# A hybrid attention and S5 layer on one core: attention's keys and the gate products behind the top-k branch, and S5's out stage in two steps

## The chip, the cores and the metric

The kernel runs on one core of a Trainium2 chip. The metric is the device time of one execution in microseconds; the median of several runs is compared. Five engines work side by side, each through its own list of instructions in order: TensorE (PE, matmuls), VectorE (DVE), ScalarE (ACT), GpSimd (POOL) and SyncE (SP), whose queue issues nearly all of the transfers here. An instruction that waits holds up everything behind it on its own engine.

## What is computed

One inference step of a layer for a prompt of 1024 tokens and a sample of 64 tokens with a cache: a normalization modulated by a condition, one combined projection, sparse attention, a complex diagonal state space model (S5), two gates, and an output projection. Cut to what matters:

```
h = rms_norm(x, g_norm) * (1 + scale) + shift
z = h @ w_in                          # split: q k v qi ki wi ga u gs ma mb
o = attention(q, top-k of the indexer's scores)
branch_a = (o * silu(ga)) @ w_attn_proj
y = S5 scan over u, then  g_lin = gelu(y) @ w_glu
branch_b = (g_lin[:512] * sigmoid(g_lin[512:]) * silu(gs)) @ w_ssm_proj
merged = sigmoid(ma) * branch_a + sigmoid(mb) * branch_b
x = x + gate * (merged @ w_out)       # gate = the last third of silu(c) @ w_mod
```

## The kernel before

All large products are made in three passes with operands split in a high and a low part (`hhi`, `hlo` for the tokens, `whi`, `wlo` for the weights; L200, L201 and L205 are the three matmuls, ACT's L155 makes `whi` and POOL's L156 `wlo`).

The part of the combined projection that is not needed at once is held as **late work**: 32 blocks of 128 columns, each in three chunks of tokens (384, 384 and 320 wide), each chunk in three steps of eight matmuls. That is nine steps to a block and 288 in all. A chunk is collected in one of two accumulators (`acc`), and the next chunk but one can begin only when it is emptied. Who empties it depends on the block, and the blocks come in this order: four of q (ACT copies to `st`, stored in `q_d`), four of u (ACT copies to `us`, L603, stored in `u_d`), fourteen of the merge gates (ACT copies to `st`, L610, stored in `ma_d` and `mb_d`), four of attention's gate (`gate_a`: ACT's sigmoid L618, then VectorE's product L619, then POOL's product L620), four of S5's gate (`gate_s`: sigmoid, VectorE's product L628, stored), and the last two of the merge gates.

A generator hands out these steps between the steps of other work, by a table of numbers: 36 steps before top-k, one step for each of attention's 75 yields (`R_ATT`), six in the gap between attention and S5 (`N_GAP`), 3.2 for each of S5's 25 yields (`R_SSM`), three for each yield of GELU (`R_GEL`), and what is left alone. So S5 begins at step 117 and ends at step 197.

The top-k indexer ends in a branch with ten arms that only VectorE enters (`tc.If`); all engines have its branch instruction in their lists. In front of that branch the program puts the keys' layout (`build_keys`, casts L265 and L266 on ACT, L267 and L268 on VectorE) and the first query block (`att_queries`: `tab`, `qt` and `qw` loads on SP, three operations on POOL, casts to `qs` on ACT and VectorE). The order of instructions on each engine follows a scheduler that keeps data dependences and may move them past each other, so what stands behind the branch in an engine's list is to be read there.

S5 (from 509 us): four times coefficients (`eb`, L271 to L276 on VectorE) are transposed (L1360), multiplied (L1367), and the result is put into `zs`; then VectorE runs the scan, seven rounds over all states and fifteen over the carries (`cmac`, L1375 to L1379), and for each of four quarters a fix (L1414 to L1420). The out stage of a quarter (`ssm_out`) issues four transfers `zq<-zs`, multiplies (L1435, L1436), copies to `yb` and issues eight stores to `y_d`. GELU reads `y_d` back (`yt`), and its result feeds the GLU. `gates` (L1171 to L1182) multiplies the condition with the last third of `w_mod` (two loads `gw` of 2 MB), reduces it with `sel` (L1178) and stores it; it is woven with GELU.

Of the kernel before, what the change touches and what calls it, by code (L numbers as in the profile page):

```python
# [47 lines left out]


N_PRE = 6  # L50
N_TOPK = 0
R_ATT = 1.0
R_SSM = 3.2
N_GAP = 6
R_GEL = 3.0
N_ATT = 14
BO = (7, 3, 4, 5, 6, 2, 1, 0, 8)
# [25 lines left out]
def hybrid_step(ctx, tc, ins, outs):  # L83
# [50 lines left out]

    acol = small.tile([P, KD, 2], F32, name="acol")
    shcol = small.tile([P, KD, 2], F32, name="shcol")
    scs = small.tile([P, KD, 2], F32, name="scs")
    nhalf = small.tile([P, 1], F32, name="nhalf")
    pool.memset(nhalf, -0.5)
    nbig = small.tile([P, 1], F32, name="nbig")  # L140
# [301 lines left out]
    for b in range(2):  # L442
        silu = act.activation(scs[:, :, b], tp[:, 0, 8 * b:8 * b + 8], AF.Silu)
    c4 = small.tile([P, KD, 4], F32R, name="c4")
    dve.tensor_copy(c4[:, :, 0:2], scs)
    c_rest = dve.tensor_tensor(c4[:, :, 2:4], scs, c4[:, :, 0:2].bitcast(F32), op=OP.subtract)

    def chain(*gens):
        for g in gens:
# [2 lines left out]
    def run(gen):  # L452
        for _ in gen:
            pass
# [8 lines left out]

    cz = sxp.tile([P, KD, 4], F32, name="cz", bufs=1)
    pool.memset(cz, 0.0)
    dve.tensor_copy(cz[:, :, 0:2], scs)
    scr = rb.tile([P, 6, 512], F32, tag="t1", name="scr")
    params = ssm_params(ssu)
    next(params)
# [196 lines left out]
    vst = kvp.tile([P, 8, 2, 2, 64], F32R, tag="v", name="vst")  # L666
    vnew = kvp.tile([64, 2, 64], F32, name="vnew")

    atq = at_ctx.enter_context(tc.tile_pool(name="atq", bufs=2, side="right"))
    tk_ctx, ix_ctx = ExitStack(), ExitStack()  # L670
    tkp = tk_ctx.enter_context(tc.tile_pool(name="tkp", bufs=1, side="right"))
    ixp = ix_ctx.enter_context(tc.tile_pool(name="ixp", bufs=2, side="right"))
# [448 lines left out]
    def steps(fn, ts):  # L1121
        for t in ts:
            fn(t)
            yield
# [31 lines left out]
    def gates():  # L1156


        sel = small.tile([P, 2], F32, name="sel")
        for b in range(2):  # L1160
            dve.tensor_reduce(sel[:, b:b + 1], ident.rearrange("p (g r) -> p g r", r=32)[:, :, b],
                              axis=mybir.AxisListType.X, op=OP.add)
        for h in range(2):
            cols = slice(2 * D + h * 512, 2 * D + h * 512 + 512)
            ps = bank1()
            w = tokp.tile([P, KD, 512], F32, tag="wtok", name="gw")
            sync.dma_start(w, w_mod[:, cols].rearrange("(k p) c -> p k c", p=P))
            yield
            for k in range(KD):
                g = 32 * (k % 4)  # L1170
                pe.matmul(ps[g:g + 2], scs[:, k, :], w[:, k], start=(k < 4), stop=(k >= 4), skip_group_check=True)  # L1171
            yield
            r = wpool.tile([P, 528], F32, tag="raw", name="grow", bufs=RAW)[:, :512]
            pool.memset(r, 0.0)
            for g in range(0, P, 32):
                act.copy(r[g:g + 2], ps[g:g + 2])
            o = bank1()[0:2]
            pe.matmul(o, sel, r, start=True, stop=True)  # L1178
            bm = wpool.tile([P, 528], F32, tag="raw", name="gbias", bufs=RAW)[0:2, :512]
            sync.dma_start(bm, ins["b_mod"][:, cols].to_broadcast([2, 512]))  # L1180
            dve.tensor_tensor(bm, o, bm, op=OP.add)
            sync.dma_start(gate_d[:, h * 512:h * 512 + 512], bm)  # L1182
            yield
# [13 lines left out]
    for _ in range(N_TOPK):  # L1197
        next(late)
    tk = topk(ixp)
    for _ in range(N_COUNT - 1 + len(BLOCKS) + 1):  # L1200
        next(tk)

    qw = wpool.tile([P, 4, P], F32, tag="ub", name="qw", bufs=1)
    pool.memset(qw, 0.0)
# [1 line left out]
    build_keys(kst, None, [(ktok[:, t], P) for t in range(8)])  # L1206
    with tc.issue_after(q_stored.ins):
        ready = att_queries(BO[0])
    run(tk)
    rest_on[0] = pool  # L1210
    ix_ctx.close()
    tk_ctx.close()

    atp_ctx = ExitStack()
    atp = atp_ctx.enter_context(tc.tile_pool(name="atp", bufs=2, side="right"))
# [206 lines left out]
    def ssm_out(q):  # L1422
        cs, tq = ca_t[q], tq_t[q]
        rs = slice(4 * q, 4 * q + 4)
        zq = ssp.tile([P, 4, 2, NCH], F32, tag="eq", name="zq")
        for j in range(2):
            for g2 in range(2):
                sync.dma_start(zq[64 * j:64 * j + 64, :, g2, :], z4[64 * g2:64 * g2 + 64, j, rs, 0:NCH])
        yb = ssp.tile([P, 8, NCH], F32, tag="yb", name="yb")
        for g0, ng in ((0, 3), (3, 3), (6, 2)):  # L1430
            ps = bank1()
            for i in range(ng):
                g = g0 + i
                o = ps[:, i * NCH:(i + 1) * NCH]
                pe.matmul(o, tq[:, g, :], uall[:, 8 * q + g, :], start=True, stop=False)  # L1435
                pe.matmul(o, cs[:, g // 2, g % 2, :], zq[:, g // 2, g % 2, :], start=False, stop=True)  # L1436
            act.copy(yb[:, g0:g0 + ng, :], ps[:, :ng * NCH].rearrange("p (g n) -> p g n", n=NCH))
        yv = y_d[P * q:P * q + P].rearrange("(g c) t n -> c g t n", c=16)
        for t in range(8):
            sync.dma_start(yv[:, :, t, :], yb[16 * t:16 * t + 16])  # L1440

    def ssm():
        for q in range(4):
            if q == 0:
                with tc.issue_after(last_mm[0].ins):
                    ssm_in(q)
            else:
                ssm_in(q)
            yield
        for i, _ in enumerate(ssm_scan()):  # L1450
            if i == OT:
                ssm_out_tables(0)
            yield
        for q in range(4):
            ssm_fix(q)
            yield
            if q < 3:
                ssm_out_tables(q + 1)
            ssm_out(q)
            yield  # L1460

    for _ in range(N_GAP):
# [20 lines left out]
    def gelu(m):  # L1483
# [4 lines left out]
        act.activation(gt[:, 1024:TOK].rearrange("p (n t) -> p t n", t=8), yt[:, :, 0:8], AF.Gelu_apprx_tanh)  # L1488
        dve.tensor_copy(ghi[:, m], gt)
        dve.tensor_tensor(glo[:, m], gt, ghi[:, m].bitcast(F32), op=OP.subtract)  # L1490
    weave(both(steps(gelu, range(4)), gates()), late, R_GEL)
    run(late)
    hT_stack.close()

# [194 lines left out]
```

## Time and profile before

| | us |
|---|---|
| median of 3 runs | 1095.76 |
| lowest, highest | 1094.28, 1097.64 |
| the profiled execution | 1094.43 |
| its span | 1092.6 |
| TensorE busy | 991.7 |
| VectorE busy | 672.8 |
| ACT busy | 461.0 |
| POOL busy | 292.2 |

The span is the time between the first and the last instruction that the profile shows; the execution takes 1.8 us more. Busy time is the sum over an engine's instructions. A busy engine can still be slow: TensorE's clock has two levels, and the profile tells the granted clock of a stretch as a share of the full one. Idle time of TensorE is put down to what released it, in the views of waits and in brackets behind an instruction in the timeline.

### The profile page before, as it was taken

What the parts mean: (1) busy time and instruction counts of PE and PEld (TensorE: products, weight loads), DVE (VectorE), ACT (ScalarE), POOL (GpSimd) and SP (SyncE); (2) the same over time, 40 slices, a digit from 0 to 9 for tenths busy, and PEclk for the clock granted to TensorE, in tenths of its full rate; (3) what the DMA queues carried; (4) which work ended last, traced back from release to release, by engine and by line L of the source; (5) the groups of instructions that cost most, each with busy time, mean ns of one, the idle gap of its engine ahead of it and who ended that gap; (6) DMA issues with size and microseconds to landing.
All of it is one profiled execution on the core that took longest, in us unless ns stands there. A gap on an engine that the chain in (4) does not pass through costs nothing. (4 is left out here: it accounts for less than half of the span.)

```text
span 1092.6 us, 16667 instructions
## 1 busy us (share of the span) xinstructions
PE 991.7 (91%) x5948; PEld 898.3 (82%) x5948; DVE 672.8 (62%) x1426; ACT 461.0 (42%) x979; POOL 292.2 (27%) x434
## 2 busy tenths in 40 slices
PE   7777999996599999999899799847999999999997
PEld 1576878996588999988789789817999999998786
DVE  6764888899688887775689950004111656665243
ACT  3675667221476676664232022126222345442122
POOL 3574202613123221211528072303312300001211
PEclk9698999998699999999999989968999999999999
DMA  8631201122122221224733265572322345544143
GB/s 301 208 91 30 76 1 53 48 81 76 40 50 68 57 49 40 80 65 86 117 87 93 53 152 126 121 233 81 92 87 94 106 129 154 162 137 145 44 145 111
DMA packets 141766, 108.41 MB, mean 99 GB/s; under 512 B 32894, under 2 KB 128680, under 8 KB 141680
## 3 DMA queue, kind: packets, MB, share of 16 engines
q1 hardware_dynamic: 140160, 105.05, 34.6%
q10 hardware_dynamic: 1232, 2.23, 0.6%
q8 instruction: 47, 0.77, 0.3%
q14 instruction: 39, 0.32, 0.1%
q0 software_dynamic: 288, 0.05, 0.0%
HBM read 77.79 MB, written 25.17 MB: 94 GB/s over the span
## 5 line engine op out<-in xcount | busy, mean ns | idle before, releaser
L200 PE MATMUL acc<-hhi,whi 128*128 128x384 f32 (+1 forms) x768 | 257.7, 340 | 24.8 <-ACT us L603 17.4
L201 PE MATMUL acc<-hlo,whi 128*128 128x384 f32 (+1 forms) x768 | 254.5, 335 | 0.0
L200 PEld LDWEIGHTS acc<-hhi,whi 128*128 128x128 f32 x768 | 147.6, 192 | 28.6 <-ACT us L603 17.7
L156 POOL TENSOR_TENSOR wlo<-raw,whi 128x512 fp32r<-128x512 f32 x64 | 88.1, 1392 | 253.4 <-ACT whi L155 187.3
L205 PE MATMUL acc<-hhi,wlo 128*128 128x384 f32 (+1 forms) x768 | 150.7, 334 | 0.3 <-POOL wlo L156 0.3
L201 PEld LDWEIGHTS acc<-hlo,whi 128*128 128x128 f32 x768 | 147.5, 192 | 1.7 <-issue 1.0
L205 PEld LDWEIGHTS acc<-hhi,wlo 128*128 128x128 f32 x768 | 130.6, 190 | 1.6 <-POOL wlo L156 0.6
L610 ACT COPY st<-acc 128x384 f32<-128x384 f32 (+1 forms) x60 | 27.6, 461 | 120.1 <-PE acc L205 108.2
L1071 DVE TENSOR_TENSOR pt<-tp,pt 128x512 fp32r<-128x512 f32 (+3 forms) x112 | 57.3, 519 | 15.0 <-ACT pt L1070 13.7
L1050 ACT ACTIVATE pm<-pm,mx 128x1024 f32<-128x1024 f32 (+8 forms) x72 | 56.1, 779 | 21.6 <-DVE mx L1043 21.2
L155 ACT CAST whi<-raw 128x512 fp32r<-128x512 f32 x64 | 37.5, 620 | 63.0 <-DMA raw<-in_w_in 39.2
L1070 ACT CAST pt<-tp 128x512 fp32r<-128x512 f32 (+3 forms) x112 | 49.4, 451 | 31.7 <-PE tp L1066 30.6
L1624 POOL TENSOR_TENSOR yh<-yh,gfin 128x512 f32<-128x512 f32 (+1 forms) x9 | 11.6, 1289 | 173.3 <-ACT xr L1620 173.3
L200 PE MATMUL acc<-wohi,mhi 128*128 128x512 f32 (+2 forms) x152 | 56.7, 377 | 0.0
L201 PE MATMUL acc<-wolo,mhi 128*128 128x512 f32 (+2 forms) x152 | 56.6, 377 | 0.0
L1066 PE MATMUL tp<-ident,pm 128*128 128x128 f32 (+2 forms) x328 | 53.7, 271 | 2.9 <-DVE pt L1071 2.8
L1043 DVE CUSTOM_DVE_ANT_0 pm<-sc,bias 128x512 f32<-128x512 f32 (+4 forms) x72 | 42.8, 594 | 15.7 <-PE sc L1040 13.8
L1040 PE MATMUL sc<-kst,qs 128*128 128x512 f32 (+3 forms) x192 | 51.8, 357 | 0.0
L619 DVE TENSOR_TENSOR sg<-acc,sg 128x384 f32<-128x384 f32 (+1 forms) x12 | 6.4, 536 | 73.6 <-DMA zq<-zs 38.8
L1083 PE MATMUL o<-pt,vst 128*128 128x256 f32 x288 | 49.1, 295 | 0.6 <-ACT pt L1070 0.3
L1066 PEld LDWEIGHTS tp<-ident,pm 128*128 128x128 f32 (+2 forms) x328 | 38.7, 140 | 10.1 <-DVE pt L1071 5.6
L707 DVE SCALAR_TENSOR_TENSOR sc<-relu,wi,sc 128x512 f32<-128x512 f32 (+5 forms) x42 | 42.6, 1017 | 3.8 <-ACT relu L705 1.0
(483 smaller groups left out, 2271.1 us busy)
## 6 DMA issues: line engine op xcount, KB each, us to landing
raw<-in_w_in SPq DMA_DIRECT2D x68, 256.0 KB
wm<-in_w_mod SPq DMA_DIRECT2D x16, 512.0 KB
xt<-in_x_prompt SPq DMA_DIRECT2D x8, 512.0 KB
gw<-in_w_mod SPq DMA_DIRECT2D x2, 2048.0 KB
raw<-in_w_out SPq DMA_DIRECT2D x16, 256.0 KB
xr<-in_x_prompt SPq DMA_DIRECT2D x16, 256.0 KB
ma_d<-st SPq DMA_DIRECT2D x16, 192.0 KB
mb_d<-st SPq DMA_DIRECT2D x16, 192.0 KB
```

Source lines behind the costliest of these rows:

```text
L156: rest_on[0].tensor_tensor(lo, raw, hi.bitcast(F32), op=OP.subtract)
L200: pe.matmul(ps, lhi(k), rhi(k), start=(k == 0), stop=False)
L201: pe.matmul(ps, lhi(k), rlo(k), start=False, stop=False)
L205: last_mm[0] = pe.matmul(ps, llo(k), rhi(k), start=False, stop=(k == nk - 1))
L707: dve.scalar_tensor_tensor(scores[b][:nq], r[:nq, :n], w, scores[b][:nq], op0=OP.mult, op1=OP.add, accum_out=sums[:nq, 0, col] if h == 4 e ...
L1040: pe.matmul(ps, self.st[:, self.h // 2, self.h % 2, :nq], self.keys[:, self.h // 4, j, c:c + m], start=(j == 0), stop=(j == 1))
L1043: dve.tensor_tensor_reduce(out=self.pm[:, c:c + m], in0=ps, in1=bias[self.b][:nq, c:c + m], op0=OP.add, op1=OP.min, scale=-0.125, scalar=t ...
L1050: act.activation(self.pm, self.pm, AF.Exp, bias=self.ng, scale=-1.0, accum_out=self.sm)
L1066: pe.transpose(tp[:rows, i, :nq], self.pm[:, c0:c0 + rows], ident[:nq, :nq])
L1070: act.copy(d0, tp[:rows, i0:i1, :nq])
L1071: dve.tensor_tensor(d1, tp[:rows, i0:i1, :nq], d0.bitcast(F32), op=OP.subtract)
L1083: last_mm[0] = pe.matmul(o, v[:rows, kt, pr // 2].rearrange("p a d -> p (a d)"), pk[:rows, j, i, :, :nq], start=(kt == 0 and j == 0), stop ...
```

## The change

Attention's keys and first query block are no longer put in front of the top-k branch but behind it: the branch is run to its end first, its pools are closed, and then 19 late steps follow in three groups of 6, 9 and 4 (`N_BR`). Between these groups `gates()` is advanced by three and two yields; its first yield, with the first `gw` load, comes right ahead of top-k. Six late steps stand ahead of top-k (`N_TOPK`). The pool of the query tiles (`atq`) is opened after those of the branch are closed. The gate product takes 32 stationary columns (of which 30 are zero) in place of 2, so that one ACT copy of 128 partitions replaces four copies and a memset. Attention hands out 1.15 late steps per yield, the gap 12, and `ssm_out` yields once between its transfers and its matmuls, so S5 has 29 yields. GELU is woven with late steps alone. S5 now begins at step 159 and ends at step 251.

```diff
-N_TOPK = 0
-R_ATT = 1.0
+N_TOPK = 6
+N_BR = (6, 9, 4)
+R_ATT = 1.15
-N_GAP = 6
+N_GAP = 12
...
-    scs = small.tile([P, KD, 2], F32, name="scs")
+    scs = small.tile([P, KD, 32], F32, name="scs")
+    pool.memset(scs, 0.0)
...
-                pe.matmul(ps[g:g + 2], scs[:, k, :], w[:, k], start=(k < 4), stop=(k >= 4), skip_group_check=True)
+                pe.matmul(ps[g:g + 32], scs[:, k, :], w[:, k], start=(k < 4), stop=(k >= 4), skip_group_check=True)
             yield
             r = wpool.tile([P, 528], F32, tag="raw", name="grow", bufs=RAW)[:, :512]
-            pool.memset(r, 0.0)
-            for g in range(0, P, 32):
-                act.copy(r[g:g + 2], ps[g:g + 2])
+            act.copy(r, ps)
...
     tk = topk(ixp)
-    for _ in range(N_COUNT - 1 + len(BLOCKS) + 1):
-        next(tk)
+    gate_steps = gates()
+    next(gate_steps)
+    run(tk)
+    ix_ctx.close()
+    tk_ctx.close()
+    atq = at_ctx.enter_context(tc.tile_pool(name="atq", bufs=2, side="right"))
+    for n, half in zip(N_BR, (3, 2, 0)):
+        for _ in range(n):
+            next(late)
+        for _ in range(half):
+            next(gate_steps, None)
 
     qw = wpool.tile([P, 4, P], F32, tag="ub", name="qw", bufs=1)
...
         ready = att_queries(BO[0])
-    run(tk)
-    rest_on[0] = pool
-    ix_ctx.close()
-    tk_ctx.close()
...
                 sync.dma_start(zq[64 * j:64 * j + 64, :, g2, :], z4[64 * g2:64 * g2 + 64, j, rs, 0:NCH])
+        yield
         yb = ssp.tile([P, 8, NCH], F32, tag="yb", name="yb")
...
-            ssm_out(q)
+            yield from ssm_out(q)
...
-    weave(both(steps(gelu, range(4)), gates()), late, R_GEL)
+    weave(steps(gelu, range(4)), late, R_GEL)
```

**ACT behind the branch, before.** The casts of the keys (`kst`) stand in front of the evictions of the `us` blocks; two of them wait for VectorE. Numbers behind a name tell buffers apart.

```order
L970 UNCONDITIONAL_BRANCH
L155 CAST whi_4162<-raw_4164 128x512 [waits DMAHW1_49,PE_49,Pool_49]
L155 CAST whi_4162<-raw_4168 128x512 [waits DMAHW2_49]
L610 COPY st_2719<-acc_2694 128x320 [waits DMAHW7_49,PE_49,Activation_49]
L265 CAST kst_2858<-tp_2859 64x512 [waits PE_49]
L266 CAST kst_2858<-tp_2859 64x512
L265 CAST kst_2858<-tp_2872 64x512 [waits PE_49]
L266 CAST kst_2858<-tp_2872 64x512
L265 CAST kst_2858<-tp_2859 64x512 [waits DVE_49]
L266 CAST kst_2858<-tp_2859 64x512
L265 CAST kst_2858<-tp_2872 64x512 [waits DVE_49]
L266 CAST kst_2858<-tp_2872 64x512
```

**ACT behind the branch, after.** The same stretch of ACT's list in the changed kernel; the last row empties the accumulator of the chunk `acc_4109`.

```order
L971 UNCONDITIONAL_BRANCH
L157 CAST whi_2748<-raw_2750 128x512 [waits DMAHW2_49,PE_49,Pool_49]
L157 CAST whi_2748<-raw_2754 128x512 [waits DMAHW3_49]
L612 COPY st_2717<-acc_2692 128x320 [waits DMAHW0_49,PE_49,Activation_49]
L605 COPY us_2745<-acc_2720 128x384 [waits DMAHW1_49,PE_49,Activation_49]
L605 COPY us_2783<-acc_2758 128x384 [waits DMAHW4_49,PE_49,Activation_49]
L157 CAST whi_4167<-raw_4169 128x512 [waits DMAHW7_49,PE_49,Pool_49]
L157 CAST whi_4167<-raw_4173 128x512 [waits DMAHW0_49]
L254 CAST qs_4385<-qt_4374 64x4x128 [waits DVE_sequencer_49,DVE_49,Pool_49]
L605 COPY us_4134<-acc_4109 128x256 [waits DMAHW5_49,PE_49,Activation_49]
```

What moved: the casts of the keys are gone from here, two evictions have come ahead, and a cast of the first query block now stands in front of the third. It waits for POOL, which in its turn waits for VectorE's sequencer and for loads.

**VectorE at the last fix of S5, before.** The second half of the last quarter's fix (`zs`, `fin`), and the first two products of `gate_a`, which empty `acc_8538` and `acc_8592`.

```order
L1414 TENSOR_TENSOR f0_8376<-car_6943,arf_6936 128x544
L1415 TENSOR_TENSOR f1_8377<-car_6943,arf_6936 128x544 [waits DVE_49]
L1416 TENSOR_TENSOR zs_6935<-zs_6935,f0_8376 128x4x136 [waits DVE_49]
L1417 TENSOR_TENSOR zs_6935<-zs_6935,f1_8377 128x4x136 [waits DVE_49]
L1418 COPY fin_6934<-zs_6935 128x2x4 [waits DVE_49]
L1419 COPY fin_6934<-zs_6935 128x2x4
L1420 MEMSET zs_6935 128x2x4 [waits DVE_49]
L619 TENSOR_TENSOR sg_8578<-acc_8538,sg_8578 128x384 [waits DMAHW4_49,DMAHW3_49,DMAHW5_49,DMAHW1_49,DMAHW7_49,DMAHW0_49,Activation_49]
L619 TENSOR_TENSOR sg_8636<-acc_8592,sg_8636 128x384 [waits DMAHW5_49,DMAHW2_49,DMAHW6_49,DMAHW1_49,Activation_49]
```

**VectorE at the last fix of S5, after.** From the first operation of the last quarter's fix on, in the changed kernel.

```order
L1418 TENSOR_TENSOR f0_8976<-car_7361,arf_7354 128x544
L621 TENSOR_TENSOR sg_8218<-acc_8178,sg_8218 128x384 [waits DMAHW3_49,DMAHW2_49,DMAHW7_49,DMAHW1_49,Activation_49]
L1422 COPY fin_7352<-zs_7353 128x2x4 [waits DVE_49]
L1423 COPY fin_7352<-zs_7353 128x2x4
L1419 TENSOR_TENSOR f1_8977<-car_7361,arf_7354 128x544
L1424 MEMSET zs_7353 128x2x4 [waits DVE_49]
L1420 TENSOR_TENSOR zs_7353<-zs_7353,f0_8976 128x4x136
L1421 TENSOR_TENSOR zs_7353<-zs_7353,f1_8977 128x4x136 [waits DVE_49]
L621 TENSOR_TENSOR sg_8272<-acc_8232,sg_8272 128x384 [waits DMAHW4_49,DMAHW0_49,Activation_49]
```

What moved: the first products of `gate_a` now stand inside the fix of the last quarter, behind the scan and the other three fixes; before they stand behind all of it.

**TensorE at the third chunk of `gate_a`, before.** The chunk `acc_8640` takes the accumulator that `acc_8538` had; two matmuls of the third out stage stand in front of it.

```order
L201 MATMUL acc_8592<-hlo_108,whi_8408 128x384
L1435 MATMUL tp_8318<-uall_6925,tq_8139 128x136 [waits DMAHW4_49,DMAHW3_49,DMAHW5_49,DMAHW2_49,DMAHW6_49,DMAHW1_49,DMAHW7_49,DMAHW0_49,PE_49]
L1435 MATMUL tp_8326<-uall_6925,tq_8139 128x136 [waits PE_49]
L205 MATMUL acc_8592<-hhi_107,wlo_8409 128x384 x8
L200 MATMUL acc_8640<-hhi_107,whi_8408 128x320 [waits DVE_49]
```

**TensorE at the third chunk of `gate_a`, after.** The chunk `acc_8276` takes the accumulator that `acc_8178` had.

```order
L202 MATMUL acc_8232<-hhi_108,whi_8079 128x384
L203 MATMUL acc_8232<-hlo_109,whi_8079 128x384
L207 MATMUL acc_8232<-hhi_108,wlo_8080 128x384 x8
L202 MATMUL acc_8276<-hhi_108,whi_8079 128x320 [waits DVE_49]
L203 MATMUL acc_8276<-hlo_109,whi_8079 128x320
```

What moved: in TensorE's list these rows stand 19 chunks behind attention's last matmuls and in front of all of S5's out stages; before, the blocks of `gate_a` begin behind the first two out stages.

## Rows read from the trace of the kernel before

**Rows 1.** The page's first part: busy us, share of the span, instructions.

```profile
PE 991.7 (91%) x5948; PEld 898.3 (82%) x5948; DVE 672.8 (62%) x1426; ACT 461.0 (42%) x979; POOL 292.2 (27%) x434
```

**Rows 2.** Waits of TensorE, 240:320, 500:560, 610:640, 700:756: sum, times, longest.

```profile
PE acc L200 <- ACT us L603: 17.4, 1, 17.4
PE acc L200 <- ACT st L610: 3.3, 1, 3.3
...
PE tp L1360 <- DVE eb L276: 5.0, 3, 2.9
...
PE tp L1436 <- DMA zq<-zs: 8.7, 2, 6.2
...
PE tp L1171 <- DMA gw<-in_w_mod: 12.3, 2, 9.2
PE tp L1436 <- DMA zq<-zs: 4.0, 1, 4.0
PE acc L200 <- ACT whi L155: 3.8, 1, 3.8
```

**Rows 3.** Stretches: length, busy (instructions) by engine, granted clock, DMA share, GB/s.

```profile
263.00:267.50 4.50, 4.50 (x18) 4.23 (x16) 4.50 (x9) 0.73 (x2) 0.00 (x0) 0.62 0.79 219
...
741.40:747.20 5.80, 5.72 (x18) 5.72 (x19) 2.63 (x2) 2.04 (x4) 4.16 (x3) 0.50 0.43 139
```

**Rows 4.** Timeline of TensorE: start, length, line, operation, [idle before <- releaser].

```profile
509.04 1.67 PE L205 MATMUL acc<-hhi,wlo 128*128 128x384 f32 x8
...
555.01 1.57 PE L205 MATMUL acc<-hhi,wlo 128*128 128x384 f32 x8
...
566.98 0.51 PE L205 MATMUL acc<-hhi,wlo 128*128 128x384 f32 x2
```

**Rows 5.** Timeline of SP, ACT and VectorE from the last out stage to GELU.

```profile
715.53 3.64 SPq L1440 DMA_DIRECT2D y_d<-yb  x8
...
739.02 2.34 SPq L1485 DMA_DIRECT2D yt<-y_d  x2
...
746.18 2.10 ACT L1487 ACTIVATE gt<-yt 128x1024 f32<-128x1024 f32 x1
...
751.34 0.73 DVE L1489 CAST ghi<-gt 128x1088 fp32r<-128x1088 f32 x1 [0.85 <-ACT gt L1488]
752.10 1.29 DVE L1490 TENSOR_TENSOR glo<-gt,ghi 128x1088 fp32r<-128x1088 f32 x1
```

**Rows 6.** Timeline of VectorE and ACT at the end of the branch.

```profile
281.26 0.68 DVE L267 TENSOR_TENSOR kst<-tp,kst 64x512 fp32r<-64x512 f32 x1 [3.23 <-issue]
...
281.98 0.58 ACT L265 CAST kst<-tp 64x512 fp32r<-64x512 f32 x1 [18.24 <-DVE kst L267]
```

**Rows 7.** Timeline of SP and POOL: the first query block, load to use.

```profile
263.79 0.37 SPq L1005 DMA_DIRECT2D qt<-q_d  x1
...
267.72 1.77 POOL L1012 TENSOR_TENSOR qt<-qt,tab 128x512 f32<-128x512 f32 x1 [5.20 <-DMA qt<-q_d]
...
270.79 1.26 POOL L1013 TENSOR_TENSOR qt<-qt,qw 128x512 f32<-128x512 f32 x1
```

**Rows 8.** Timeline of VectorE: scan, carries, first operations of the first and last fix.

```profile
555.20 1.23 DVE L1375 TENSOR_TENSOR t<-zs,arf 128x544 f32<-128x544 f32 x1 [4.16 <-ACT zs L1371]
...
560.17 1.23 DVE L1375 TENSOR_TENSOR t<-zs,arf 128x544 f32<-128x544 f32 x1
...
565.09 2.07 DVE L1375 TENSOR_TENSOR t<-zs,arf 128x544 f32<-128x544 f32 x1
...
600.40 0.23 DVE L1375 TENSOR_TENSOR t<-car,arf 128x32 f32<-128x32 f32 x1
...
615.79 0.72 DVE L1414 TENSOR_TENSOR f<-car,arf 128x544 f32<-128x544 f32 x1
...
634.26 0.76 DVE L1414 TENSOR_TENSOR f<-car,arf 128x544 f32<-128x544 f32 x1
```

**Rows 9.** The stretch of scan and fixes: columns as in rows 3.

```profile
555.20:635.00 79.80, 71.07 (x425) 69.67 (x425) 78.14 (x143) 14.54 (x29) 34.12 (x27) 0.94 0.31 84
```

More of the change, by code (lines that the diff above doesn't have):

```diff
@@ L444, in hybrid_step @@
     c4 = small.tile([P, KD, 4], F32R, name="c4")
-    dve.tensor_copy(c4[:, :, 0:2], scs)
-    c_rest = dve.tensor_tensor(c4[:, :, 2:4], scs, c4[:, :, 0:2].bitcast(F32), op=OP.subtract)
+    dve.tensor_copy(c4[:, :, 0:2], scs[:, :, 0:2])
+    c_rest = dve.tensor_tensor(c4[:, :, 2:4], scs[:, :, 0:2], c4[:, :, 0:2].bitcast(F32), op=OP.subtract)
     def chain(*gens):
@@ L465, in hybrid_step @@
     pool.memset(cz, 0.0)
-    dve.tensor_copy(cz[:, :, 0:2], scs)
+    dve.tensor_copy(cz[:, :, 0:2], scs[:, :, 0:2])
     scr = rb.tile([P, 6, 512], F32, tag="t1", name="scr")
@@ L667, in hybrid_step @@
     vnew = kvp.tile([64, 2, 64], F32, name="vnew")
-    atq = at_ctx.enter_context(tc.tile_pool(name="atq", bufs=2, side="right"))
     tk_ctx, ix_ctx = ExitStack(), ExitStack()
```

## The prediction

> **What bounds the kernel now.** I read the page's busy times first: TensorE is busy 991.7 of 1092.6 us [rows 1], so the end is set by its work plus the time it loses. The change adds no product: the same 288 late steps (eight matmuls each, nine steps to a block of 128 columns) and the same sixteen gate products are placed elsewhere, the latter with 32 stationary columns instead of 2 and as many moving columns. So the whole question is what TensorE loses in waits and at half clock, before and after. I read that from the waits of TensorE in four stretches, then from the granted clock in the stretches behind each wait.
>
> In A, behind the top-k branch (250 to 318 us), it idles 22.6 us: 17.4 for the eviction of a `us` block on ACT, 3.3 for a `st` eviction [rows 2], and 1.9 in a smaller wait. In B, the start of S5 (509 to 556), about 7.1, of which 5.0 for the coefficient tiles `eb` of VectorE [rows 2]. In C, the first out stage (620 to 636), 8.7 for the carried states `zq` [rows 2]. In D, the end of S5 with the gate products woven into GELU (704 to 754), 25.0: 12.3 for the gate weights, 4.0 for `zq`, 3.8 for a weight cast [rows 2], and 4.9 in two smaller waits, both at the gate's reduction. Sum 63.4 us.
>
> After each pause the clock is at its lower level (1.2 GHz) for a while: ten stretches, of which the first and the last stand in [rows 3]. Busy time times (1 - granted clock) gives 4.5 x 0.38 = 1.7 and 5.72 x 0.50 = 2.9 for these two, and read the same way 6.1 for A, 1.7 for B, 2.8 for C and 9.2 for D, 19.8 in all. So before loses 28.7 in A, 8.8 in B, 11.5 in C, 34.2 in D: **83.2 us**, the most that the change can win.
>
> **C and D: the gain.** The gate products leave D for the place behind the branch, so 12.3 + 4.9 us of waits go; their loads (2 MB each) are now issued before top-k and behind the branch. `zq` was issued right before the matmuls that read it; now a yield lies between. A block of nine late steps, three column chunks, takes 566.98 - 555.01 = 11.97 us [rows 4]: 4.22 for each chunk of 384 columns, 3.53 for that of 320. By the order of the instructions four to five chunks, 16 to 21 us, lie between a quarter's fix and the matmuls that read its `zq`; the longest wait was 6.2 [rows 2]. I cost C at nothing: the cover is these chunks. If it went, 6 to 9 us would come back.
>
> D has a new price. The late steps are used up earlier (19 at the branch, 86 instead of 75 in attention, 12 instead of 6 in the gap, 92 instead of 80 in S5), so behind the last out stage only six chunks, 24 us, stand in front of the GLU, against 33 before. Its input comes by a chain: eight `y_d` stores (3.6 us to issue), the `yt` load (issued at 739.02, used by ACT at 746.18, so 7.2), then four GELU blocks of 2.1 + 0.3 on ACT, and the cast and the split of the last (0.73 + 1.29) on VectorE [rows 5]. The stores wait for `yb` and the first loads also stand behind two `ma`/`mb` stores on SP's queue. That makes 30.5 to 32 us against 24 to 26: a wait of some 6, and 2 at half clock. D: 34.2 becomes **8** (3 to 12).
>
> **A: one wait for another.** The keys' casts no longer stand on ACT in front of the `us` evictions, which is what made TensorE wait: ACT waited 18.24 us for VectorE's L267, and that stood behind the branch (L267 starts at 281.26, with 3.23 us of issue before it) [rows 6]. But the first query block is moved as well, and its tiles come from a pool that is opened only after the branch's pools are closed. So SP's `tab` load now waits for the branch. Queued behind it on SP are the `qt` and `qw` loads, the `u_d` stores and the next weights; on ACT the cast `qs<-qt` stands in front of the eviction that TensorE needs (the order shows it). The chain: the branch's end at 278 to 281.3; load to use 267.72 - 263.79 = 3.9; three operations on POOL to 270.79 + 1.26, that is 4.3 [rows 7]; a cast 0.6 and the eviction 0.4. TensorE resumes at 287.5 to 291, I take 290.7 (the end of the issue time in [rows 6]). It runs dry later than now (267.5), by one chunk of 3.5, one of 4.2 and half of the gate products, 1.7: at 277. So 13.8 idle (10.5 to 15) in place of 17.4, and as before 3.3 and 1.3 ahead of it, about 6 at half clock; 1.9 may go or stay. A: 28.7 becomes **26** (22 to 31). The second query block's casts stand in front of the next eviction too; with two accumulators TensorE has 8 to 11 us of cover for a chain of the same 10 to 11, so I take nothing for it.
>
> **B and the scan: the new wait.** With 12 steps ahead and 92 in S5, the blocks of `gate_a` (late steps 198 to 234) come inside S5; in before S5 ended at step 197. Their eviction needs VectorE (the product at L619, `sg<-acc`), and the order shows the first such product behind seven rounds of the long scan, fifteen of the carries, the fixes of three quarters and the first operation of the fourth. TensorE has two accumulators: it must wait with the third `gate_a` chunk until VectorE comes to that product. When? In before VectorE reached the same operation at 634.26 to 635.0, with TensorE's last attention matmuls at 509.04 [rows 4, 8]: +126, and the product +0.6. VectorE's start of the scan (555.20, +46) is set by `par` and by TensorE's transposes; by the after order I get +45, so it stays. TensorE's work in after from attention's end to that chunk: 13 chunks x 4.22 + 6 x 3.53 = 76, transposes and small products 15: 91. So TensorE waits 126.5 - 91 = **35** of which about 3 fall at S5's start, and loses 3 more at half clock: 38 where B lost 8.8. In before this wait is not there, because `gate_a` came after the scan. The bounds: of VectorE's chain part is delay by POOL. A round of the scan takes 560.17 - 555.20 = 4.97 undisturbed, seven 34.8; they ended at 600.4, in 45.2; an operation at 565.09 took 2.07 in place of 1.23. The carries took 615.79 - 600.4 = 15.4 against 15 x 0.85 = 12.8, and the fixes lost 2.2 [rows 8]: some 15 in all. If POOL is quiet in after, the loss is 23; if it disturbs twice as much, 53.
>
> **The sum.** Lost after: A 26 + scan 38 + C 0 + D 8 = 72, against 83.2: a gain of 11 to 12. The profiled execution took 1094.43 (span 1092.6), so 1082.7; the median is 1.33 above it: **1084.0**.
>
> **The rivals.** First, *a quiet POOL*: TensorE's wait also stops the late weights' splits on POOL, so VectorE runs the scan undisturbed. For it: the last splits at 630 would not come. Against: most splits and the tables come before TensorE stops. Price 15: 1069. Chance 0.15.
>
> Second, *everything does what it says*: no wait behind the scan, since VectorE may stand earlier than I count. A 26, B 9, D 8: a gain of 40, 1056. The order speaks against it, as VectorE runs its row in sequence. Chance 0.07.
>
> Third, *slower*: the scan is held longer. In before POOL was busy 34.1 us while VectorE ran from 555.2 to 635 [rows 9], and VectorE lost 15. Were it held for the whole of POOL's time, 19 more would be lost, and the kernel would take 1103. For it: with the tables of a quarter and the gate products of POOL (L620) in the same stretch, POOL is not less loaded. It decides from a scan 15 us longer. Against it: at 565.09 the loss was 0.84, less than one of POOL's operations there. The Trainium skill ("SBUF — State Buffer", section "Who interferes with whom") says that a VectorE instruction with two SBUF inputs contends with a GpSimd instruction that reads SBUF, and that the second fully blocks until the first is done. By that rule the time is this rival's, 1103; the trace agrees that there is a delay (2.07 for 1.23), but shows less than a full block. Chance 0.19.
>
> Fourth, *a pile-up behind the branch*: the second query block's casts, the gate's `grow` copy and the evictions stand in one row on ACT, and each waits for loads on an SP queue that begins only at 278. Were the second chain to repeat the first's idle time by two thirds, 9, it gives 1093. Chance 0.13.
>
> **How the numbers follow.** Forecast 0.46, with its own range 1076 to 1092; the four rivals 0.15, 0.07, 0.19, 0.13. A measurement here tells 0.3%, 3.3 us, from no change: 1092.5 to 1099.0. Faster: 0.44 of the forecast, the first two rivals 0.22, four tenths of the last 0.05: 0.71. Same: 0.02 + half of the last 0.07 + a fifth of the third 0.04: 0.13. Slower: 0.16. The range 1063 to 1102 leaves out the second rival and the upper half of the third, 0.17.
>
> **What would show it.** The waits of TensorE should list one of about 30 us for the `sg` product of VectorE inside S5, one of about 14 for `us` behind the branch, none of over 2 for `gw` or `zq`, and some 6 before the first large GLU product. VectorE should reach its first `sg` product some 126 us after attention's last matmuls. If the wait for `sg` is under 15 the second rival is right, and the forecast's largest term wrong; if `gw` still appears, SP's queue was late, and A is mis-sized; if attention, which has no wait of TensorE worth a row now, shows new idle time, its cover at 86 steps was misjudged.

## The result, and the profile after

The changed kernel took 1082.3 us (median of 4, 1077.0 to 1084.3), the kernel before beside it 1096.1. The ratio is 0.987, 95% interval 0.983 to 0.991: faster by 13.8 us. The forecast was 1084.0.

The profiled execution of after took 1083.0 us with a span of 1081.2, 11.4 less than before's 1092.6. The busy times on its page:

```profile
PE 987.0 (91%) x5948; PEld 891.0 (82%) x5948; DVE 673.0 (62%) x1426; ACT 457.5 (42%) x973; POOL 290.6 (27%) x433
```

The same 5948 matmuls as in [rows 1] are busy 4.7 us less, and the mean granted clock is 0.958 in place of 0.951: fewer of them run at half clock. The other 6.7 us are idle time of TensorE: 1092.6 - 991.7 = 100.9 before, 1081.2 - 987.0 = 94.2 after.

The waits of TensorE after, sum, times and longest, answer [rows 2]:

```profile
PE acc L202 <- DVE sg L621: 29.4, 2, 28.4
PE tp L590 <- POOL zA L243: 9.4, 5, 3.9
PE acc L202 <- ACT us L605: 7.6, 1, 7.6
PE acc L202 <- ACT st L612: 4.7, 2, 3.4
PE big L203 <- DVE glo L1495: 4.0, 2, 3.1
...
PE big L202 <- DVE ghi L1494: 2.3, 1, 2.3
...
PE tp L1364 <- DVE eb L278: 2.0, 1, 2.0
```

`gw`, `zq` and `whi` are gone, and `us` has shrunk from 17.4 to 7.6. One wait is new, the longest of all: 28.4 us for VectorE's product `sg<-acc`. The timeline shows it (start, length, line, operation, idle before and its releaser): TensorE first, then VectorE from the scan's last rounds to the product.

```profile
556.42 1.68 PE L207 MATMUL acc<-hhi,wlo 128*128 128x384 f32 x8
...
650.88 1.57 PE L207 MATMUL acc<-hhi,wlo 128*128 128x384 f32 x8
680.86 0.63 PE L202 MATMUL acc<-hhi,whi 128*128 128x320 f32 x1 [28.40 <-DVE sg L621]
```

```profile
613.80 0.72 DVE L1382 TENSOR_TENSOR zs<-zs,t 128x272 f32<-128x272 f32 x1
...
635.40 4.19 DVE L1382 TENSOR_TENSOR zs<-zs,t 128x272 f32<-128x272 f32 x1
...
680.25 0.55 DVE L621 TENSOR_TENSOR sg<-acc,sg 128x384 f32<-128x384 f32 x1
```

VectorE does its scan, its carries and the fixes in one row and takes `sg<-acc` at 680.25, while TensorE has stood still since 652.46.

TensorE's granted clock behind the five pauses, with length, busy time (instructions), clock, DMA share and GB/s:

```profile
263.00:268.50 5.50, 5.50 (x21) 0.59 0.51 130
286.40:292.20 5.80, 5.71 (x15) 0.57 0.58 114
580.80:586.50 5.70, 5.68 (x45) 0.70 0.19 64
680.80:686.50 5.70, 5.64 (x28) 0.72 0.21 55
823.00:834.00 11.00, 7.38 (x22) 0.54 0.06 19
```

Behind each pause, of 2 us or of 28, the mean lies between the two levels of 1.2 and 2.4 GHz (0.5 and 1.0): a part of the stretch ran at the lower one. By busy time times (1 - clock), that is 2.3 + 2.5 behind the branch, 1.7 + 1.6 in S5 and 3.4 before the GLU.

### The profile page after: what moved, and what is told of

The parts are those of the page before. It is cut to its first block, busy times and chain, and to the rows that moved or that the text cites. A ratio compares the mean times of both kernels' runs of the same rounds, so it can differ in the third digit from the quotient of the medians.

```text
span 1081.2 us, 16676 instructions
## 1 busy us (share of the span) xinstructions
PE 987.0 (91%) x5948; PEld 891.0 (82%) x5948; DVE 673.0 (62%) x1426; ACT 457.5 (42%) x973; POOL 290.6 (27%) x433
## 4 chain that ended last, share of the span: by engine, by line
PE 62%; DVE 22%; ACT 4%; issue 4%; POOL 3%; DMA 2%; SPq 2%; DVEq 0%; POOLq 0%; ACTq 0%
PE acc L202 12%; PE acc L207 12%; PE acc L203 11%; PE o L1084 4%; PE big L207 3%; PE big L203 3%; PE big L202 3%; PE tp L1067 3%; PE sc L1041 3%; DVE gt L910 2%; DVE near_v L917 2%; DVE sc L708 1%; PE big L695 1%; DVE t L1379 1%; DVE below L919 1%
## 5 line engine op out<-in xcount | busy, mean ns | idle before, releaser
L207 PE MATMUL acc<-hhi,wlo 128*128 128x384 f32 (+1 forms) x768 | 148.2, 332 | 0.9 <-POOL wlo L158 0.9
L1013 POOL TENSOR_TENSOR qt<-qt,tab 128x512 f32<-128x512 f32 (+1 forms) x9 | 11.0, 1226 | 124.1 <-DMA qt<-q_d 117.2
```

What stands on the lines that cost most here:

```text
L207: last_mm[0] = pe.matmul(ps, llo(k), rhi(k), start=False, stop=(k == nk - 1))
```

## Experiments: is the wait for `sg` what the prediction says

All times stand against the kernel before, run on the same chip (about 1097 us). Line numbers shift by a few between kernels.

**A quiet POOL.** (`e4_quiet_pool`) The forecast holds that POOL delays VectorE's scan. This kernel leaves POOL's `wlo` splits out for seven late blocks (17 to 23), and with them the low part of those blocks' weights:

```
-                    nxt = load_T(*jobs[i + 1][:2], KD)
+                    nxt = load_T(*jobs[i + 1][:2], KD, quiet=17 <= i + 1 <= 23)
```

> The changed kernel with POOL's split of the weights left out for the seven blocks around the scan (the third pass of these blocks uses the high part again, so the low part of their weights is left out of the result). The scan's seven rounds took 47 us in the changed kernel against 35 at the undisturbed rate. My theory, VectorE is held while POOL works: without the splits the first sg product comes 6 to 10 us earlier behind attention's end than the 123.8 now, and the wait for sg falls from 28.4 to 19 to 23. Rival, the slow operations have another cause (transfers, TensorE): 123.8 and 28.4 stay within 2 us.

1076.4 us in a single run. The wait, by the list of waits:

```profile
PE acc L209 <- DVE sg L628: 21.7, 1, 21.7
```

6.7 us shorter, as expected. The first `sg` product came 115.9 us after attention's last late products (558.23), against 680.25 - 556.42 = 123.8 in after. So the place and the delay by POOL are as forecast, and the splits carry 7 to 8 us of it. The seven rounds alone gained more:

```profile
603.89:640.10 36.21, 36.21 (x223) 35.81 (x222) 35.76 (x35) 7.39 (x15) 8.90 (x10) 1.00 0.29 82
```

They took 36.2 us, near the undisturbed 34.8, against 47.0 in after (columns: length, then the busy time of PE, PEld, DVE, ACT and POOL). Some 4 us came back in the carries (17.0 in place of 12.9), where POOL's table operations now fall.

**`gate_a` two blocks later.** (`e1_gate_a_later`) If the wait is only that of `gate_a`'s eviction, more independent blocks ahead of it should fill it:

```
-N_ATT = 14
+N_ATT = 16
```

> The changed kernel with one number changed: the last two blocks of the merge gates come in front of the blocks of gate_a in place of behind gate_s (N_ATT 16 for 14), so gate_a begins 18 late steps, some 24 us, later. My theory: TensorE's wait of 28.4 us in S5 is the order on VectorE alone, so it falls to 0 to 8 (the first zq then becomes the wait, 1 to 6, since only seven chunks more stand ahead of it), and the kernel takes 1055 to 1063. Rival, the wait is VectorE's capacity (the scan is late whatever stands ahead): the wait moves to another place with 20 us or more, and the time stays at 1078 to 1085. Rival, the steps lost at the end matter more: the GLU's start waits 10 us longer.

1078.8 us, ratio 0.983 (0.981 to 0.986): a miss, with the time that the first rival names. The wait for `sg` went, and another took its place. The list of waits:

```profile
PE acc L202 <- ACT st L612: 22.4, 2, 18.8
...
PE big L202 <- ACT whip L157: 6.2, 1, 6.2
```

ACT's row in that stretch, and SP's:

```profile
676.97 0.62 ACT L157 CAST whi<-raw 128x512 fp32r<-128x512 f32 x1 [22.46 <-DMA raw<-in_w_in]
```

```profile
648.98 0.38 SPq L164 DMA_DIRECT2D raw<-in_w_in  x1
671.41 1.26 SPq L1432 DMA_DIRECT2D zq<-zs  x2
672.77 0.55 SPq L164 DMA_DIRECT2D raw<-in_w_in  x1
```

SP issues nothing for 22 us. At the head of its queue stands the load of `zq`, which waits for VectorE to finish a quarter's fix, and the second half of the next weights stands behind it. ACT's cast waits for these weights, TensorE for the eviction queued behind the cast. Both waits, that for `sg` and that for the weights, hang on VectorE's one row behind the scan: `zq` is issued when the first quarter's fix ends (in after at 670.22), the `sg` product stands 10 us further on (680.25). So two waits lie on top of each other, and taking away one uncovers the other.

**The queue as well.** (`e9_later_zq_behind`) The `zq` loads are placed behind the last store of a projected block, `gate_a` is two blocks later as above:

```
+        with tc.issue_after(stored[0].ins):
+            for j in range(2):
+                for g2 in range(2):
+                    sync.dma_start(zq[...], z4[...])
```

> The run with gate_a later, and in addition the zq transfers of the out stage are queued on SP behind the store of the last late chunk that was handed out, so that no weights and no stores stand behind a transfer that waits for VectorE. There the wait of 28.4 for VectorE's sg had gone, and one of 18.8 for a st eviction stood in its place, with SP issuing nothing from 649 to 671. My theory now: one block of the late work's weights stood behind zq on SP's queue, so that TensorE was held by a second row at nearly the same time. With it moved: no wait over 8 us in S5, the sum of the waits there 3 to 12, and 1062 to 1071. Rival, VectorE's capacity: the sg wait returns with 15 us or more, 1075 to 1081.

1079.1 us, ratio 0.983 (0.981 to 0.985): a miss on the time. The waits:

```profile
PE acc L202 <- DVE sg L621: 8.2, 1, 8.2
...
PE big L202 <- ACT whip L157: 6.6, 1, 6.6
PE tp L1442 <- DMA zq<-zs: 6.4, 1, 6.4
```

The 18.8 is gone, and 8.2 + 6.4 came back in S5; the 6.6 before the GLU's products stayed. By the page TensorE idles 1077.1 - 991.4 = 85.7 us, 3.5 less than in the run before (1076.7 - 987.5), but it is busy 3.9 longer, so nothing is won. The time is the rival's, the wait for `sg` isn't. If the order is right now, late products to put in the way are what is missing; the next section tries that.

## Experiments: the steps that attention takes

**1.0 late steps per step of attention** (`e11_even_steps`), as in before, instead of 1.15. This undoes one number of the change:

```
-R_ATT = 1.15
+R_ATT = 1.0
```

> The changed kernel with one number changed back towards a smaller share: attention is given 1.0 late product steps per step of its own instead of 1.15, so fewer of the 288 steps (about 11 of 86) are used there, and these come later, behind S5's scan or in front of the GLU. Theory (the length of the waits is only a matter of how many late steps are left when VectorE starts the scan and when the last out stage ends): attention's end comes some 11 x 1.33 = 15 us earlier and VectorE reaches its first sg product as much earlier, and the gate_a chunk that waits for it comes no earlier against attention's end than before, so the wait inside S5 stays, but shrinks only if the steps of S5 are cut from the same budget: between 13 and 29 us; the six or seven us before the GLU go, since 15 us more late products stand there. Time 1058 to 1076. Rival (attention is bounded by its own chain of score, softmax and transposes, so that fewer late steps leave TensorE idle there): attention shows 10 us or more of new idle time and the time is 1079 to 1088.

1061.3 us, ratio 0.968 (0.966 to 0.969): 21 us faster than after by one number. Attention loses nothing by it. Its stretches (columns as in [rows 3], TensorE alone), from 320 us to its last product with the values, in after and here:

```profile
320.27:556.23 235.96, 232.56 (x1565) 1.00 0.21 57
```

```profile
320.00:540.67 220.67, 218.31 (x1474) 1.00 0.22 56
```

With 86 steps TensorE idles 3.4 us, with 75 2.4: the eleven more steps covered no wait. That product ends 15.6 us earlier, and the eleven steps now lie where TensorE has nothing else. The waits before the GLU are gone, and those in S5 are 17.2 and 3.6 in place of 28.4:

```profile
662.93 0.69 PE L202 MATMUL acc<-hhi,whi 128*128 128x384 f32 x1 [17.18 <-ACT st L612]
...
672.31 0.41 PE L202 MATMUL acc<-hhi,whi 128*128 128x320 f32 x1 [3.55 <-DVE sg L621]
```

The rival, idle time in attention, has fallen. By the page TensorE idles 1059.7 - 983.0 = 76.7 us in this kernel, against 94.2 in after, and is busy 4.0 us less: together the 21.5 us between the spans.

**The two waits of S5, one at a time, at 1.0 steps.** First the queue alone (the edit of `zq` above on this kernel, `e12_even_zq_behind`), then `gate_a` alone (`N_ATT` 16 on this kernel, `e13_even_gate_a_later`).

> The kernel of e11_even_steps (1.0 late steps per step of attention), and the load of the carried states zq issued only behind the last store of a projected block, so that the loads of the next weights no longer stand behind it on SP's queue. In e11_even_steps TensorE waited 17.2 us for an st eviction while SP issued nothing from 630.5 to 654.2, where zq waited for VectorE's fix of a quarter. Theory (that wait is the queue's head, and at 1.0 steps VectorE is near enough to its products): the 17.2 goes, a wait for sg of 5 to 12 takes part of its place, since VectorE's first sg product comes no earlier; net 5 to 12 us: 1049 to 1056. Rival (as in e9_later_zq_behind, what the queue gives back is lost again behind VectorE's chain and at the zq matmuls): waits for sg and zq together 14 or more, time 1058 to 1063.

> The kernel of e11_even_steps, and gate_a two blocks later (16 blocks of ma and mb ahead of it), the queue as it was. Theory (the longest wait in S5 is now the queue's head: zq waiting for VectorE holds the weights): the wait for st or whi stays, 14 to 22 us, and the sg wait of 3.6 goes; 1055 to 1062. Rival (more independent blocks are all that S5 lacked): no wait over 6 us inside S5, 1045 to 1051.

1063.4 us (ratio 0.970, 0.968 to 0.972) and 1065.1 us (0.973, 0.969 to 0.977): neither is faster than 1061.3. The first is at the rival's end: its wait is on `sg` alone, longer than the theory's 5 to 12. The second kept its wait as the theory had it, but its time lies above the theory's range. What each left, the queue's kernel first:

```profile
671.98 0.64 PE L202 MATMUL acc<-hhi,whi 128*128 128x320 f32 x1 [22.70 <-DVE sg L621]
```

```profile
664.70 0.69 PE L202 MATMUL acc<-hhi,whi 128*128 128x384 f32 x1 [17.50 <-ACT st L612]
```

With the queue mended TensorE waits for `sg`, with `gate_a` moved it waits for the weights. That is the either-or which the row of SP suggested.

**Both together** (`c1_all`), with the query tiles in a pool of their own that is opened ahead of the branch's pools:

```
-R_ATT = 1.15
+R_ATT = 1.0
-N_ATT = 14
+N_ATT = 16
+    atl = at_ctx.enter_context(tc.tile_pool(name="atl", bufs=1, side="right"))
...
-        qt = atq.tile([P, 4, P], F32, tag="qt", name="qt", bufs=1)
+        qt = atl.tile([P, 4, P], F32, tag="qt", name="qt", bufs=1)
...
+        with tc.issue_after(stored[0].ins):
```

> The changed kernel with gate_a later, zq queued behind the last chunk's store, the first query block's load tiles early, and attention handing out 1.0 late steps per yield for 1.15 (11 steps more are left for the scan and the end). My theory: TensorE's work up to the first gate_a chunk then covers VectorE's 124 to 134 us, and 36 steps are left behind S5, so the wait in front of the GLU (9 us) goes too: no wait over 5 us behind 290 us, 1042 to 1056. Rival, attention is slower with fewer steps or the waits come back elsewhere: 1060 to 1075.

1048.2 us, ratio 0.956 (0.953 to 0.959): 34 us faster than after and 48 faster than before. The longest waits behind the top-k branch:

```profile
PE acc L202 <- ACT whi L157: 4.0, 2, 3.7
PE acc L202 <- ACT us L605: 3.8, 2, 3.5
PE tp L1443 <- DMA zq<-zs: 3.6, 1, 3.6
PE acc L202 <- ACT st L612: 3.5, 1, 3.5
```

TensorE idles 1045.6 - 986.0 = 59.6 us. Of the 17 less than in the kernel with 1.0 steps alone, the waits in S5 gave the most (17.2 + 3.6 became 3.6, now for `zq`), the wait for `us` 6 (9.9 became 3.8); 5 came back before the GLU, 3.7 of it for `whi`. How the two mended waits do without the early tiles was not run.

## Experiments: behind the branch and in the tail

**The keys alone back in front of the branch** (`e8_keys_front`), all else as in after:

```
+    for _ in range(N_COUNT - 1 + len(BLOCKS) + 1):
+        next(tk)
+    kst = rb.tile([P, 2, 2, 1024], F32R, tag="t2", name="kst")
+    build_keys(kst, None, [(ktok[:, t], P) for t in range(8)])
     run(tk)
```

> The changed kernel with the keys' layout alone back in front of the branch (the query block stays behind it). My theory: the casts of the keys stand on ACT in front of the us evictions again and wait for VectorE, so TensorE waits 10 to 14 us from 268 on, and then runs through the chunks that covered the query block; the wait of 7.6 shrinks or goes, the waits for the keys at attention's start (0.7) go: 1083 to 1090. Rival, the keys' place is worth nothing, since either chain ends at the branch's end: within 3 us of 1082.

1076.7 us, ratio 0.982 (0.980 to 0.984): a miss, by the medians 5 to 6 us faster than after, whose interval (0.983 to 0.991) its own just touches. The wait for `us` fell to 0.3, and a wait of 6.0 ahead of the gate's products came instead:

```profile
282.01 3.64 PE L1172 MATMUL tp<-gw,scs 128*32 128x512 f32 x16 [6.03 <-issue]
```

```profile
281.21 0.69 DVE L269 TENSOR_TENSOR kst<-tp,kst 64x512 fp32r<-64x512 f32 x1
```

The gate's products take an accumulator `tp` as the keys do, and start 0.1 us after VectorE is through with this one, behind the branch. So it fits that the keys' chain still holds TensorE, in another row; the view names no releaser. The first score of attention came at 308.1 us against 312.6, and attention's last matmul ended 7 us earlier (549 against 556). So the title's first part, the keys behind the branch, won nothing and by the medians cost time; what gained was the removal of the gate products from the tail. On the kernel of 1048.2 the same edit (`c2_all_keys_front`) gave nothing:

> The kernel of c1_all (gate_a two blocks later, zq behind the store, the query tiles in a pool of their own, 1.0 late steps per step of attention) with the keys built in front of the branch again, as in e8_keys_front. Theory (the keys behind the branch cost a little everywhere, as e8_keys_front showed with 5 us): the us wait of 3.5 behind the branch goes, attention begins earlier, and the time is 1041 to 1046. Rival (that gain came only through the waits behind attention, which c1_all has removed already, or the keys' six us of issue on TensorE in front of the gate products cancel it): 1046 to 1053.

1047.7 us, ratio 0.955 (0.953 to 0.956), the same as 1048.2: the rival's. There it takes 3.5 of `us` away and brings 7.7 in front of the gate's products.

**The query tiles alone in a pool of their own** (`e2_tiles_early`), the edit of `atl` above. It tells whether the first query load waits for the branch's pools.

> The changed kernel with the tiles of the first query block's loads (qt, tab) in a pool of their own that is opened ahead of the branch's pools; the qs tiles stay behind it. My theory: the wait of 7.6 us for the us eviction behind the branch is the load chain that begins at the branch's end, so with qt ready the cast runs at the branch's end and the wait falls to 0 to 2, with 1 to 2 us less at half clock: 1071 to 1076. Rival, ACT's row is held by something else (VectorE's end of the branch): the wait stays at 5 or more and the time within 3 us of 1082.

1080.0 us, ratio 0.983 (0.980 to 0.986). The wait for `us` shrank from 7.6 to 4.0 us in two pieces, not to 0 to 2. The first loads are issued at 265 us in place of 277, so they did wait for the branch's pools. ACT's cast then waits for VectorE's last operation of the branch, the rival's reason, and the time is the rival's too:

```profile
281.49 0.62 ACT L254 CAST qs<-qt 64x512 fp32r<-64x512 f32 x1 [8.14 <-DVE bias L791]
```

That operation ends at 281.4, in after at 276.7. The query block's POOL operations now run at 269.2 to 273.6, beside the end of the branch on VectorE, where the same four small copies took 3.17 us in place of 0.72:

```profile
271.68 3.17 DVE L955 COPY fl<-turned 1x14 f32<-1x14 f32 x4
```

So it fits that the earlier loads made the branch itself later, which ate much of what they gave; no run took the two apart. The difference to after lies inside both intervals, and what the edit is worth alone isn't settled.

**The gate products back in GELU** (`e5_gates_in_gelu`), the keys and the rest as in after:

```
-    gate_steps = gates()
-    next(gate_steps)
...
-    weave(steps(gelu, range(4)), late, R_GEL)
+    weave(both(steps(gelu, range(4)), gates()), late, R_GEL)
```

> The changed kernel with the gate products back in GELU's weave, as before; all numbers of steps stay. My theory: the gate products' move is the larger part of what D lost, 12.3 us for their weights and 5 at the reduction, so those waits come back in large part, while the wait in front of the GLU (9 us) is partly covered by them; behind the branch TensorE has 3.5 us less work, so the wait for us grows from 7.6 to 9 to 11. 1089 to 1099. Rival, at the end there are six chunks in front of the GLU in any case and the gate's loads hide behind them: 1080 to 1086.

1092.9 us, ratio 0.997 (0.995 to 0.999). Moving these sixteen products is worth some 10 us of the 13.8 that the change won: most of it. The waits behind it:

```profile
PE acc L202 <- ACT us L605: 10.6, 2, 10.4
PE tp L1172 <- DMA gw<-in_w_mod: 9.3, 1, 9.3
```

**The out stage in one step** (`e3_no_yield`), its yield taken away:

```
-        yield
         yb = ssp.tile([P, 8, NCH], F32, tag="yb", name="yb")
...
-            yield from ssm_out(q)
+            ssm_out(q)
```

> The changed kernel with the out stage of S5 in one step again, as before (no yield between the zq transfers and their matmuls), which also gives S5 25 yields for 29 and leaves 12 more late steps for the end. My theory: the first zq is hidden behind the wait for sg, the others come back with 3 to 6 us each (8 to 15 in sum with the half clock), while the wait in front of the GLU (9 us and 3 at half clock) goes: 1077 to 1086. Rival, zq stays hidden since VectorE is through with all fixes by then: only the gain at the end is left, 1068 to 1073.

1081.8 us, ratio 0.987 (0.984 to 0.989), the same as after, no wait for `zq` in the list and `sg` at 28.4. So the yield is worth nothing here. Neither half of the theory came: `zq` stayed hidden, and the waits before the GLU (`glo` 4.0, `ghi` 2.3) stayed too, since TensorE's stretch between the last out stage and the GLU is 25 us in both kernels; that the time lies in the theory's range is chance. What hides `zq` without the yield is TensorE's order. The first quarter's last `zq` transfer and the first matmul that reads it:

```profile
683.14 0.59 SPq L1432 DMA_DIRECT2D zq<-zs  x1
```

```profile
699.81 0.40 PE L1440 MATMUL tp<-zq,cs 128*128 128x136 f32 x2
```

Between them lie 17 us of late products, and in the other quarters 21, 8 and 8 from the first transfer (in after 21, then 21, 4.5 and 9). TensorE's wait for `sg` is over by then (679.4), so it isn't that wait which covers `zq`.

## Why the prediction held, and where it did not

**The total** was right (1084.0 against 1082.3), and so was the list of waits to look for: one for `sg` of about 30 in S5, none over 2 for `gw` or `zq`, one for `us` (7.6, forecast about 14), some 6 before the GLU (7.6 in four pieces). Its last step takes 11.7 off where the terms give 83.2 - 72 = 11.2, which changes nothing. Of its terms two came out lower and one higher. Read as in the prediction, after loses A 19, scan 35, C 0, D 12, and 1.7 in attention, which had no term: 67 us, not 72. But 83.2 - 67 = 16 is 4 to 5 more than the spans' 11.4. Most of that lies in the half-clock terms, sums over stretches picked by hand: they fell by 8.3, from 19.8 to 11.5, while the page's busy time fell by 4.7. The early waits for `zA` took another 1.4 (9.4 against 8.0 before). So that the total lies within 2 us is in part luck: the terms together came out 5 lower than forecast (7 and 3 lower, 4 and 2 higher), the count of the losses overstates the gain by about as much, and the two cancel.

**A** was forecast at 26 and came out at 19 (13.9 idle, 4.8 at half clock). The step that failed is the branch's end: I took the load of `qt` to follow at 278 to 281.3, with the 3.2 us of issue time in [rows 6]. VectorE's last operation of the branch and SP's first load stand here:

```profile
276.47 0.26 DVE L790 TENSOR_SCALAR bias<-gts 128x384 bf16<-128x384 bf16 x1
```

```profile
276.76 0.34 SPq L1008 DMA_DIRECT2D tab<-in_rope_feat  x1
```

The load starts 0.3 us after the branch's last operation does, so it does not wait for those 3.2 us of issue time. TensorE also ran dry later, at 278.9 instead of 277. The chain itself was right: load to use 280.46 - 277.15 = 3.3, three operations to 285.4, cast and eviction to 286.5. Nor did it take anything away, in after's surroundings, that the keys' casts no longer stand ahead of the evictions: with the keys alone in front again TensorE waits 0.3 for `us` and 6.0 ahead of the gate's products, in place of 7.6, and the time is no longer than after's.

**B and the scan** were forecast at 38 and came out at 34.7 (31.4 idle, 3.3 at half clock). The product came 123.8 us after attention's last late products, forecast 126.5, and TensorE's wait began 96 after, forecast 94 (91 of work and 3 of pause). Of VectorE's delay by POOL the forecast had 15 us. The window of the scan's seven rounds, with busy time of PE, PEld, DVE, ACT and POOL, reads:

```profile
603.35:650.40 47.05, 47.05 (x289) 46.66 (x288) 46.60 (x36) 11.31 (x21) 26.38 (x20) 1.00 0.33 90
```

Seven undisturbed rounds of 4.97 are 34.8, so some 12 us went to 26.4 us of POOL's work; the carries (12.9, undisturbed 12.8) lost nothing. The third rival, 19 more for the whole of POOL's time, needed more than that and did not come. The Trainium skill ("SBUF — State Buffer", section "Who interferes with whom") calls the shared port pair an exclusive lock; read as a full block for all of POOL's time that would be 26.4; the trace shows less than half of it.

**C** was forecast at nothing, and is. Half of the reason was right: the cover is late products, as forecast. The other half was wrong: I put their place there down to the yield, and without the yield TensorE's order has them there too.

**D** was forecast at 8 (3 to 12) and came out at 12.3: 8.9 idle and 3.4 at half clock. Of the 30.5 to 32 us of its chain the rows that it names add up to 22.4; for the rest, put on the stores' waits, it shows no row. In after the chain takes 36, from the last out stage's last matmul (793.6) to the last split of GELU's output (829.8). The term that was mis-sized is VectorE's cast and split of that output, 0.73 + 1.29 in [rows 5]. After, they run beside POOL's four operations that split `oT`:

```profile
819.90 3.46 DVE L1495 TENSOR_TENSOR glo<-gt,ghi 128x1088 fp32r<-128x1088 f32 x1
823.28 3.01 DVE L1494 CAST ghi<-gt 128x1088 fp32r<-128x1088 f32 x1
826.33 3.48 DVE L1495 TENSOR_TENSOR glo<-gt,ghi 128x1088 fp32r<-128x1088 f32 x1
```

```profile
819.26 12.91 POOL L1541 TENSOR_TENSOR olo<-oT,ohi 128x1088 fp32r<-128x1088 f32 x4 [11.28 <-PE acc L207]
```

With 1.0 steps POOL comes to its four operations only at 808.18, behind the last split, which is quick again, and no wait is left before the GLU:

```profile
800.05 1.29 DVE L1495 TENSOR_TENSOR glo<-gt,ghi 128x1088 fp32r<-128x1088 f32 x1
```

**What the prediction did not see** is the price of one number. It noted that attention takes 86 steps instead of 75 and priced that at 6 us before the GLU. Undone, it gives 21 us: 7.6 of idle time before the GLU, some 9 in S5, 1 in attention, and 4.0 of busy time (mean granted clock 0.967 in place of 0.958). And it priced the wait for `sg` as if nothing stood behind it; there was a second wait for the weights under it, at SP's queue, which its sum did not contain.

## What to carry to other kernels

Independent products that fill waits are a stock: give them to a stage only as far as its idle time in the trace asks for them, since a stage that idles 2 us out of 220 returns nothing for more, and the stage at the end pays. Before a long wait is taken away, look what each engine and each queue does in the same stretch; if a second wait hangs on the same row, both have to go at once: either edit alone won nothing here. In a queue that issues in order, a load that waits for an engine holds everything behind it, so it belongs behind the loads of the next weights.

## What was not expected of the hardware

VectorE's operations beside POOL's took up to nearly six times as long as alone: the same 128x272 operation of the scan 0.72 us and 4.19 us, the 128x1088 cast 0.73 and 3.01. The delay of one operation says little about a stage: over the scan's rounds it was some 12 us for 26.4 us of POOL's time, and in the quiet kernel 1.4 for 8.9. And the wait for `sg` was 28.4 us in after and in four of its variants (tiles early, no yield, gates in GELU, keys in front), though attention ended up to 7 us apart: it hangs on what lies between attention and the product.
